# Two right-hand sums of a Strassen-Winograd down-projection formed on VectorE ahead of their store, instead of by adding DMA transfers ahead of their use

## The chip, the cores and the metric

The kernel runs on one core of a Trainium2 chip. The metric is the device time of one execution in microseconds (us). Times are medians of a few runs; profiles are of one execution each. The engines are named as in the profile: PE is TensorE's matmul and PEld its weight load, DVE is VectorE, ACT is ScalarE, POOL is GpSimd, SP is SyncE, which here only issues DMA transfers.

## The reference, cut to what matters

The model has two layers on an input of 1024 frames by 1024 channels, in float32. Each layer has a mixer and then a gated MLP with a short convolution. The change touches the MLP only:

```python
def conv_ffn(h, w_up, conv_w, conv_b, w_down):
    u = h @ w_up                                   # 1024 x 5632
    up = jnp.pad(u, ((0, 0), (CONV_WIDTH - 1, 0), (0, 0)))
    conv = conv_b
    for j in range(CONV_WIDTH):                    # width 3, along the frames
        conv = conv + conv_w[j] * up[:, j:j + s]
    a, g = jnp.split(conv, 2, axis=-1)
    return (jax.nn.silu(a) * g) @ w_down           # (1024 x 2816) @ (2816 x 1024)
```

The result is added to the residual stream.

## The kernel before, in words

Everything is held with channels on the 128 partitions and the 1024 frames along a row. A float32 matmul is made of three: each operand is split into a high part, rounded by a ScalarE copy, and a low part, a VectorE subtraction, and high times high, high times low and low times high are accumulated. Such a split is one ScalarE and one VectorE instruction (`split_block`, L1193 to L1197, for one 128x512 block).

**Up-projection** (`ffn`, L1011 on). The 2816 hidden channels are 22 tiles of 128. For tile i the kernel computes a pair, the `a` tile and the `g` tile, by one level of the Strassen-Winograd scheme: seven products instead of eight (`Pair`, L966 to L1005: P1, P5, P6, P2, P7, P4, P3, twelve 128x512 matmuls each), and VectorE adds that build the four output quarters (L990, L995, L1001, L1005) and scale them (L964). L1005 needs the end of P3; P3 accumulates into a bank that L995 must have read. VectorE and ScalarE also prepare the next pair's weights (L907 to L918), and then the convolution of the finished pair runs on ScalarE (L1038) and VectorE (L1039, L1041), followed by SiLU (L1171) and the product with the gate. The pairs 0 and 1 are computed plainly.

**What the down-projection needs.** It also uses the Strassen-Winograd scheme. Hidden tiles 2j and 2j + 1 form a block row j, with the two halves of the frames as block columns: B11 and B12 from the even tile, B21 and B22 from the odd one. The right-hand sides of the seven products are B11, T1 = B12 - B11, T2 = T3 + B11, T3 = B22 - B12, B22, T4 = T2 - B21, and B21. The end of each pair (L1174 to L1188) computes what is stored to device memory. An even pair leaves the product in `even` (L1175), T1 (L1176), and stores B11 and T1. An odd pair leaves B21 and B22 in `ca` (L1182), U = B11 - B21 in the first half of `cg` (L1183) and T3 in the second half (L1184), and stores `ca` (`b2`, L1186) and `cg` (`ut3`, L1187), 512 KB each. `even` is a single buffer; `ca` and `cg` come from three buffers used in turn. T2 and T4 are stored nowhere: T2 is T3 + B11, and T4 is T3 + U.

**Down-projection** (`down`, L1199 on). The order of the work is (product, j) with j from 0 to 10 inside and the products P1, P5, P6, P3, P7, P4 outside: six phases of eleven steps, 66 steps a layer, each of twelve 128x512 matmuls (`step`, L1260 to L1267). A last part with plain matmuls finishes the rows that need the seventh product. A step's operands are made by `prep` (L1243), called three steps ahead (`LEAD`, L1299): `fetched` (L1209) loads the right-hand block into one of four `rb` buffers from SP, and, where `right` (L1241) lists two sources, issues a second transfer from GpSimd that adds the second source to what has landed (L1213). That is so in P6 (T3, then B11) and in P4 (T3, then U). The left-hand block is made by `left` (L1218) from weights, in part kept from earlier phases. Both blocks are split by `split_block`. Between the steps further transfers are issued: residual rows (`load_x`), in P6 at j = 2 and j = 6 two groups of weights for the last part (`last_left`, L1287, 512 KB and 192 KB each), and in P7 and P4 the B21 blocks (`last_right`, L1275).

**What sets the order.** TensorE's instructions, and in the down-projection SP's too, stand in the order of the program. On the other engines a planner at build time orders them with a simulated timeline; each engine then runs its own list in order and waits on semaphores.

Of the kernel before, what the change touches and what calls it, by code (L numbers as in the profile page):

```python
# [12 lines left out]
F32 = mybir.dt.float32  # L13
R32 = mybir.dt.float32r
AF = mybir.ActivationFunctionType
ALU = mybir.AluOpType

P = 128
T = 1024
# [38 lines left out]
def trunk_kernel(  # L58
# [22 lines left out]
    nc = tc.nc  # L81
    V, S, G, PE = nc.vector, nc.scalar, nc.gpsimd, nc.tensor
# [9 lines left out]
    dram = ctx.enter_context(tc.tile_pool(name="dram", bufs=1, space=bass.MemoryType.DRAM))  # L92

    def slot(dtype, name):
        return xpool.tile([P, T], dtype, tag="x", name=name)
# [915 lines left out]
    def ffn(layer, nm, after, ow, mixt, onward=None):  # L1011
# [5 lines left out]
        T0, T1 = HALVES  # L1017
# [18 lines left out]
        def conv(m, u, c):  # L1036
            b = C_CONV + (layer * 2 * FT + m) * 4
            S.activation(c, u, AF.Identity, scale=pcol(b + 2), bias=pcol(b + 3))  # L1038
            V.scalar_tensor_tensor(c[:, 1:], u[:, :T - 1], pcol(b + 1), c[:, 1:],  # L1039
                                   op0=ALU.mult, op1=ALU.add)  # L1040
            V.scalar_tensor_tensor(c[:, 2:], u[:, :T - 2], pcol(b), c[:, 2:],  # L1041
                                   op0=ALU.mult, op1=ALU.add)
# [63 lines left out]
        even = slot(F32, "even")  # L1106
        cs_ = [slot(F32, "c") for _ in range(3)]
        blocks = []
        ready = []

        def first_down():

            raw = wpool.tile([P, T], F32, tag="wraw", name="wraw", bufs=1)
            for j, t in enumerate((w.raw_g, s12, s34, raw)):
                nc.sync.dma_start(t[:, T0], wdn[layer, 2 * j][:, T0])
                nc.sync.dma_start(t[:, T1], blocks[j]["B11"])
                ready.append((split_block(t[:, T0]), split_block(t[:, T1])))

        for i in range(FT):
            nx = i + 1 < FT  # L1120
            ca, cg = cs_[2 * i % 3], cs_[(2 * i + 1) % 3]
            if i == 0:
                ua, ug = us[0], us[1]
            elif i == 1:
                ua, ug = us[2], us[0]
                for cs, b in zip(HALVES, ps):
                    V.tensor_tensor(ug[:, cs], b, rstd_bc[:, cs], op=ALU.mult)
            else:
                further = i + 2 < FT
                if i == 2:  # L1130
                    p = Pair(i)
                    p.P1()
                ua, ug = p.ua, p.ug
                if not nx:
                    first_down()
                p.P5()
                if nx:
                    sums(i + 1)
                    split_a11(i + 1)
                if further:  # L1140
                    load_a(i + 2)
                p.P6()
                if nx:
                    split_s12()
                p.P2()
                scaled(ua[:, T0], T0)
                p.P7()
                scaled(ug[:, T1], T1)
                p.P4()
                p.D21()  # L1150
                if nx:
                    split_a22()
                if further:
                    load_g(i + 2)
                scaled(ug[:, T0], T0)
                q, p = p, None
                if nx:
                    p = Pair(i + 1)
                    p.P1()
                q.P3()  # L1160
                if nx:
                    split_s34()
                if further:
                    load_s4(i + 2)
                scaled(ua[:, T1], T1)
            if i == 1:
                for ld in loads:
                    ld(i + 2)
            conv(FT + i, ug, cg)
            conv(i, ua, ca)  # L1170
            S.activation(ca, ca, AF.Silu)  # L1171


            if i % 2 == 0:  # L1174
                V.tensor_tensor(even, ca, cg, op=ALU.mult)  # L1175
                V.tensor_tensor(ca[:, T0], even[:, T1], even[:, T0], op=ALU.subtract)  # L1176
                b11, t1 = (dram.tile([P, 512], F32, tag=f"{n}{layer}_{i}", name=n) for n in ("b11", "t1"))
                nc.sync.dma_start(b11, even[:, T0])
                nc.sync.dma_start(t1, ca[:, T0])
                blocks.append({"B11": b11, "T1": t1})  # L1180
            else:
                V.tensor_tensor(ca, ca, cg, op=ALU.mult)  # L1182
                V.tensor_tensor(cg[:, T0], even[:, T0], ca[:, T0], op=ALU.subtract)  # L1183
                V.tensor_tensor(cg[:, T1], ca[:, T1], even[:, T1], op=ALU.subtract)  # L1184
                b2, ut3 = (dram.tile([P, T], F32, tag=f"{n}{layer}_{i}", name=n) for n in ("b2", "ut3"))
                nc.sync.dma_start(b2, ca)  # L1186
                nc.sync.dma_start(ut3, cg)  # L1187
                blocks[-1].update(B21=b2[:, T0], B22=b2[:, T1], U=ut3[:, T0], T3=ut3[:, T1])  # L1188
        ev.close()

        down(layer, blocks, ready, after, onward)

    def split_block(src):  # L1193
        t = hpool.tile([P, T], R32, tag="h", name="blk")
        S.copy(t[:, 0:512], src)  # L1195
        V.tensor_sub(t[:, 512:T], src, t[:, 0:512].bitcast(F32))  # L1196
        return t  # L1197

    def down(layer, blocks, ready, after, onward):  # L1199
# [5 lines left out]
        T0, T1 = HALVES  # L1205
        NJ = FT // 2
        w = [(wdn[layer, 2 * j], wdn[layer, 2 * j + 1]) for j in range(NJ)]

        def fetched(tag, src, add=None, bufs=4):  # L1209
            t = dn.tile([P, 544 if tag == "rb" else 512], F32, tag=tag, name=tag, bufs=bufs)[:, 0:src.free_size()]  # L1210
            nc.sync.dma_start(t, src)
            if add is not None:
                G.dma_start(t, add, accum_op=ALU.add)  # L1213
            return t

        a11, s = [None] * NJ, [None] * NJ

        def left(n, j):  # L1218

            (lo_, hi_) = w[j]  # L1220
            if n == "P1":
                return a11[j]
            if n == "P5":
                s[j] = fetched("rs", hi_[:, T1], bufs=NJ)
                t = fetched("rw", lo_[:, T1])
                V.tensor_tensor(s[j], s[j], t, op=ALU.add)
                return s[j]
            if n == "P6":
                V.tensor_tensor(s[j], s[j], a11[j], op=ALU.subtract)
                return s[j]  # L1230
            if n == "P4":
                return fetched("rw", hi_[:, T1])
            t = fetched("rw", hi_[:, T0] if n == "P3" else lo_[:, T1])
            if n == "P3":
                V.tensor_tensor(t, t, s[j], op=ALU.subtract)
            else:
                V.tensor_tensor(t, a11[j], t, op=ALU.subtract)
            return t


        right = {"P1": ("B11",), "P5": ("T1",), "P6": ("T3", "B11"), "P3": ("B22",), "P7": ("T3",), "P4": ("T3", "U")}  # L1241

        def prep(n, j):  # L1243
            if n == "P1" and j < len(ready):
                return ready[j]
            rb = fetched("rb", *(blocks[j][b] for b in right[n]))
            if n == "P1":
                load_a11(j)
            return split_block(left(n, j)), split_block(rb)

        def load_a11(j):
            a11[j] = fetched("ra", w[j][0][:, T0], bufs=NJ)
# [50 lines left out]
        for n, j in order[:LEAD]:  # L1303
            ops[n, j] = prep(n, j)
# [55 lines left out]
        if onward is not None:  # L1360
            with norm.behind():
                n = wov0.shape[2]
# [25 lines left out]

    norm.sq_tile = lambda: slot(F32, "nsq")
    ffn(0, n0, lambda m: norm.add(x[m], HALVES if m == KT // 2 - 1 else None, m), ws, [mix[k] for k in last], onward)  # L1390


    ev = ExitStack()
    op = ev.enter_context(tc.tile_pool(name="odd", bufs=1, reuse_waits="tile"))
# [235 lines left out]
    for hd in range(GH):  # L1630
# [36 lines left out]

    nnorm = NormBlocks(1, C_FFN1, lambda: slot(F32, "nacc"), lambda: slot(F32, "nsq"))
    ffn(1, nnorm, lambda m: [nc.sync.dma_start(yT[m * P:(m + 1) * P, cs], x[m][:, cs]) for cs in HALVES],
        ow, mixt)  # L1670

# [63 lines left out]
```

## Time and profile before

| | |
|---|---|
| median of 3 runs | 2199.06 us (2197.35 to 2202.14) |
| the profiled execution's own time | 2199.35 us |
| its span in the profile | 2197.7 us |
| mean granted TensorE clock | 0.996 |
| up-projection pairs, layer 0 / layer 1 | about 483 to 881 us / 1571 to 1968 us |
| six down-projection phases, layer 0 / layer 1 | 881.4 to 1071.3 us / 1968.5 to 2162.4 us |
| bytes moved by DMA | 280.3 MB in 126,201 packets |

All times inside the run are counted from the span's start. In a group's row the numbers behind `x` are the count, the busy time in us and the mean of one in ns, then the engine's idle time just before the group and who ended it. In a timeline the columns are start, length, engine, line, operation, output and inputs; a bracket gives the idle time before it and its releaser. In a list of DMA issues the last number is the median time from issue to landing in us. A matmul of 512 columns shows some 390 ns, but successive ones overlap.

### The profile page before, as it was taken

How to read it: one execution, taken by the hardware profiler on the slowest of the kernel's cores; microseconds unless marked ns; L12 is line 12 of the kernel's file. 1: busy time of each engine (PE TensorE's matmuls, PEld its weight loads, DVE VectorE, ACT ScalarE, POOL GpSimd, SP SyncE). 2: the span in 40 equal slices, each digit the busy share in tenths (PEclk: the TensorE clock that was granted, in tenths of full speed). 3: DMA queues.
4: the chain of work that ended last, by engine and by line, in shares of the span. 5: the costliest groups of instructions: out<-in, count | busy, mean ns of one | idle time of the engine just before them, and what ended most of it. 6: DMA issues, size and time to landing. Idle time of an engine off the chain costs nothing.

```text
span 2197.7 us, 28082 instructions
## 1 busy us (share of the span) xinstructions
PE 2150.8 (98%) x10384; PEld 1767.0 (80%) x10384; DVE 1664.8 (76%) x2458; ACT 1093.1 (50%) x1705; POOL 162.1 (7%) x188
## 2 busy tenths in 40 slices
PE   8999989999999999999999999999999999999998
PEld 7889878888878888778887878787788888887776
DVE  5687688698989899777736655557898998987763
ACT  6666566464444444344546362637544444443441
POOL 2240120000000000010000000000000000000110
PEclk9999999999999999999999999999999999999999
DMA  4132332353444434987501111105343444449885
GB/s 152 49 107 87 94 112 94 119 130 106 130 119 126 124 116 124 350 216 233 169 21 40 38 49 38 49 30 145 105 124 116 123 122 120 124 157 327 222 239 157
DMA packets 126201, 280.31 MB, mean 128 GB/s; under 512 B 13408, under 2 KB 27360, under 8 KB 126064
## 3 DMA queue, kind: packets, MB, share of 16 engines
q1 hardware_dynamic: 112528, 251.25, 34.9%
q0 software_dynamic: 13536, 27.27, 7.0%
q8 instruction: 81, 1.33, 0.2%
q14 instruction: 56, 0.46, 0.1%
HBM read 208.21 MB, written 54.53 MB: 120 GB/s over the span
## 4 chain that ended last, share of the span: by engine, by line
PE 61%; DMA 15%; DVE 15%; issue 4%; ACT 4%; SPq 1%; POOL 0%; DVEq 0%; ACTq 0%; POOLq 0%
PE lin L936 10%; PE z L936 7%; PE lin L153 4%; PE lin L155 4%; PE lin L157 4%; DMA rb<-ut 4%; PE t L936 3%; PE d L936 3%; DMA rw<-in_wdn 3%; DVE blk L1196 2%; PE z L157 2%; PE z L153 2%; PE z L155 2%; DMA raw_g<-in_wup 2%; DMA wraw<-in_wup 2%
## 5 line engine op out<-in xcount | busy, mean ns | idle before, releaser
L1038 ACT ACTIVATE c<-u,prm 128x1024 f32<-128x1024 f32 x88 | 109.1, 1244 | 86.7 <-DVE u L964 79.1
L1266 PE MATMUL lin<-blk 128*128 128x512 f32 x396 | 118.6, 400 | 14.0 <-ACT blk L1195 8.6
L1196 DVE TENSOR_TENSOR blk<-rb,blk 128x512 fp32r<-128x512 f32 x124 | 85.1, 686 | 53.9 <-ACT blk L1195 53.4
L153 PE MATMUL lin<-h_hi,whi 128*128 128x512 f32 x288 | 114.2, 432 | 6.6 <-ACT whi L139 6.0
L1039 DVE SCALAR_TENSOR_TENSOR c<-u,prm,c 128x1023 f32<-128x1023 f32 x88 | 112.3, 1278 | 8.5 <-ACT c L1038 8.5
L1195 ACT CAST blk<-rb 128x512 fp32r<-128x512 f32 x124 | 76.6, 618 | 81.2 <-DMA rb<-ut 44.0
L936 PE MATMUL d<-T,a 128*128 128x512 f32 x480 | 115.4, 389 | 0.0
L1041 DVE SCALAR_TENSOR_TENSOR c<-u,prm,c 128x1022 f32<-128x1022 f32 x88 | 112.3, 1276 | 0.0
L1266 PE MATMUL t<-blk 128*128 128x512 f32 x396 | 112.0, 391 | 0.0
L1266 PE MATMUL d<-blk 128*128 128x512 f32 x396 | 111.9, 391 | 0.0
L1266 PE MATMUL z<-blk 128*128 128x512 f32 x396 | 111.6, 390 | 0.0
L964 DVE TENSOR_TENSOR u<-u,rstd_bc 128x512 f32<-128x512 f32 x160 | 107.8, 684 | 0.4
L936 PEld LDWEIGHTS d<-T,a 128*128 128x128 f32 x480 | 90.1, 188 | 18.7
L155 PE MATMUL lin<-h_lo,whi 128*128 128x512 f32 x288 | 104.4, 398 | 0.7 <-DVE h_lo L264 0.7
L1266 PEld LDWEIGHTS lin<-blk 128*128 128x128 f32 x396 | 73.0, 189 | 39.8 <-ACT blk L1195 13.2
L157 PE MATMUL lin<-h_hi,wlo 128*128 128x512 f32 x288 | 104.2, 398 | 0.0
L936 PE MATMUL z<-blk,s34h 128*128 128x512 f32 x320 | 101.3, 398 | 1.4 <-DVE u L995 1.4
L936 PE MATMUL z<-blk,s12h 128*128 128x512 f32 x320 | 100.9, 396 | 0.0
L936 PE MATMUL lin<-T,s34h 128*128 128x512 f32 x320 | 99.5, 392 | 0.8 <-ACT tm L986 0.8
L936 PE MATMUL t<-blk,whi 128*128 128x512 f32 x320 | 99.6, 392 | 0.0
L936 PE MATMUL lin<-blk,whi 128*128 128x512 f32 x320 | 99.5, 392 | 0.0
L936 PE MATMUL lin<-T,s12h 128*128 128x512 f32 x320 | 99.4, 391 | 0.0
(516 smaller groups left out, 6021.0 us busy)
## 6 DMA issues: line engine op xcount, KB each, us to landing
wraw<-in_wup SPq DMA_DIRECT2D x44, 512.0 KB, 3.7
rw<-in_wdn SPq DMA_DIRECT2D x88, 256.0 KB, 4.7
raw_g<-in_wup SPq DMA_DIRECT2D x40, 512.0 KB, 3.8
rb<-ut SPq DMA_DIRECT2D x66, 256.0 KB, 4.4
b<-c SPq DMA_DIRECT2D x22, 512.0 KB, 2.6
ut<-c SPq DMA_DIRECT2D x22, 512.0 KB, 3.8
s<-in_wup SPq DMA_DIRECT2D x40, 256.0 KB, 2.6
s<-s POOLq DMA_DIRECT2D x40, 256.0 KB, 4.4
```

Of the source, the lines that this page charges most:

```text
L153: PE.matmul(out[i], wh, ah[i], start=first, stop=False)
L155: PE.matmul(out[i], wh, al[i], start=False, stop=False)
L157: PE.matmul(out[i], wl, ah[i], start=False, stop=last)
L936: PE.matmul(ps, w, m, start=first and k == 0 and n == 0, stop=k == 3 and n == 2, skip_group_check=True)
L964: V.tensor_tensor(dst, dst, rstd_bc[:, cs], op=ALU.mult)
L1038: S.activation(c, u, AF.Identity, scale=pcol(b + 2), bias=pcol(b + 3))
L1039: V.scalar_tensor_tensor(c[:, 1:], u[:, :T - 1], pcol(b + 1), c[:, 1:], op0=ALU.mult, op1=ALU.add)
L1041: V.scalar_tensor_tensor(c[:, 2:], u[:, :T - 2], pcol(b), c[:, 2:], op0=ALU.mult, op1=ALU.add)
L1195: S.copy(t[:, 0:512], src)
L1196: V.tensor_sub(t[:, 512:T], src, t[:, 0:512].bitcast(F32))
L1266: PE.matmul(ps, l, m, start=first and j == 0 and i == 0, stop=j == NJ - 1 and i == 2, skip_group_check=True)
```

## The change

T2 and T4 are formed on VectorE at the end of each odd pair, where U and T3 have just been made. `cg` then holds T4 beside T3 and is stored as `t43`. T2 is formed in place in the first half of `even` and stored as a further 256 KB tensor, `t2`. In the down-projection every product has one right-hand source, and `fetched` loses its adding transfer. The sums have the same terms as before.

```diff
                 V.tensor_tensor(cg[:, T0], even[:, T0], ca[:, T0], op=ALU.subtract)
                 V.tensor_tensor(cg[:, T1], ca[:, T1], even[:, T1], op=ALU.subtract)
-                b2, ut3 = (dram.tile([P, T], F32, tag=f"{n}{layer}_{i}", name=n) for n in ("b2", "ut3"))
+                V.tensor_tensor(cg[:, T0], cg[:, T0], cg[:, T1], op=ALU.add)
+                V.tensor_tensor(even[:, T0], even[:, T0], cg[:, T1], op=ALU.add)
+                b2, t43, t2 = (dram.tile([P, n], F32, tag=f"{s}{layer}_{i}", name=s)
+                               for s, n in (("b2", T), ("t43", T), ("t2", 512)))
                 nc.sync.dma_start(b2, ca)
-                nc.sync.dma_start(ut3, cg)
-                blocks[-1].update(B21=b2[:, T0], B22=b2[:, T1], U=ut3[:, T0], T3=ut3[:, T1])
+                nc.sync.dma_start(t43, cg)
+                nc.sync.dma_start(t2, even[:, T0])
+                blocks[-1].update(B21=b2[:, T0], B22=b2[:, T1], T4=t43[:, T0], T3=t43[:, T1], T2=t2)
...
-        def fetched(tag, src, add=None, bufs=4):
+        def fetched(tag, src, bufs=4):
             t = dn.tile([P, 544 if tag == "rb" else 512], F32, tag=tag, name=tag, bufs=bufs)[:, 0:src.free_size()]
             nc.sync.dma_start(t, src)
-            if add is not None:
-                G.dma_start(t, add, accum_op=ALU.add)
             return t
...
-        right = {"P1": ("B11",), "P5": ("T1",), "P6": ("T3", "B11"), "P3": ("B22",), "P7": ("T3",), "P4": ("T3", "U")}
+        right = {"P1": "B11", "P5": "T1", "P6": "T2", "P3": "B22", "P7": "T3", "P4": "T4"}
...
-            rb = fetched("rb", *(blocks[j][b] for b in right[n]))
+            rb = fetched("rb", blocks[j][right[n]])
```

## Prediction

> **What bounds the kernel.** I read the head of the profile page first, then the matmul timeline of the two down-projections, the table of stretches cut at their phase borders, the list of DMAs and, last, VectorE's timeline in an up-projection.
>
> ```profile
> span 2197.7 us, 28082 instructions
> PE 2150.8 (98%) x10384; PEld 1767.0 (80%) x10384; DVE 1664.8 (76%) x2458; ACT 1093.1 (50%) x1705; POOL 162.1 (7%) x188
> L1266 PE MATMUL lin<-blk 128*128 128x512 f32 x396 | 118.6, 400 | 14.0 <-ACT blk L1195 8.6 <-DVE blk L1196 5.4
> ```
>
> TensorE is busy for all but 47 us, so a gain has to come out of matmuls that wait or run slowly. The costliest matmul group is L1266, the down-projections' step, and its waits are for `split_block` (L1195, L1196). Below, each row is one phase of eleven steps (132 matmuls): first P1, P5, P6, P3, P4 of layer 0, then P5, P6, P3, P4 of layer 1. A phase ends where the next one's first matmul starts. The columns are the length, the busy time (and instructions) of PE, PEld, DVE, ACT and POOL, the granted clock, the DMA share and GB/s.
>
> ```profile
> 881.36:911.30 29.94, 29.94 (x134) 24.77 (x132) 21.39 (x31) 12.23 (x19) 0.00 (x0) 1.00 0.98 344
> 911.30:943.80 32.50, 31.58 (x134) 24.30 (x132) 28.30 (x46) 13.09 (x23) 2.46 (x3) 1.00 0.92 311
> 943.80:980.81 37.01, 33.26 (x133) 25.70 (x132) 22.49 (x35) 17.12 (x30) 7.09 (x9) 0.95 0.93 225
> 980.81:1010.73 29.92, 29.92 (x133) 24.77 (x132) 26.09 (x43) 15.89 (x28) 0.00 (x0) 1.00 0.69 223
> 1040.65:1071.27 30.62, 30.40 (x133) 24.70 (x132) 23.44 (x38) 15.30 (x28) 5.79 (x7) 1.00 0.94 260
> 1998.47:2030.41 31.94, 31.21 (x134) 24.39 (x132) 27.74 (x46) 12.65 (x23) 2.60 (x3) 1.00 0.92 318
> 2030.41:2066.53 36.12, 31.65 (x134) 24.54 (x132) 21.28 (x33) 16.22 (x28) 6.92 (x8) 1.00 0.87 214
> 2066.53:2096.45 29.92, 29.92 (x133) 24.77 (x132) 26.23 (x43) 15.78 (x28) 0.00 (x0) 1.00 0.70 227
> 2126.37:2162.43 36.06, 32.20 (x134) 24.45 (x132) 24.38 (x39) 15.58 (x28) 6.05 (x7) 1.00 0.86 234
> ```
>
> P3 is the yardstick: 29.92 us, so 2.72 us a step, without a wait. P6 and P4 do the same matmuls and take longer, and these are the two phases whose right-hand sum is made by an adding transfer. Their DMA engines are nearly as full as in P1 while they move a third less. The next rows say why. The first four are of 945 to 980 us: queue, packets, megabytes, share of the engines, then the issues with KB and time to landing. The other four are of the whole run.
>
> ```profile
> q1 hardware_dynamic: 5077, 5.46, 52.9%
> q0 software_dynamic: 1280, 2.33, 40.1%
> rb<-b POOLq DMA_DIRECT2D x8, 256.0 KB, 6.2
> wraw<-in_wdn SPq DMA_DIRECT2D x2, 512.0 KB, 7.8
> rb<-ut SPq DMA_DIRECT2D x66, 256.0 KB, 4.4
> L1213 POOL DMA_DIRECT2D rb<-b x22 | 19.1, 880 | 213.7 <-DVE rs L1229 86.5 <-DVE blk L1196 86.2 <-DMA rb<-ut 36.8
> L1195 ACT CAST blk<-rb 128x512 fp32r<-128x512 f32 x124 | 76.6, 618 | 81.2 <-DMA rb<-ut 44.0 <-DMA rb<-b 33.5 <-PE d L1266 2.1
> L1196 DVE TENSOR_TENSOR blk<-rb,blk 128x512 fp32r<-128x512 f32 x124 | 85.1, 686 | 53.9 <-ACT blk L1195 53.4
> ```
>
> The adding transfers take 40.1% of the engines for 2.33 MB where plain ones take 52.9% for 5.46 MB: 1.8 times the price per byte. They also come one behind another. An `rb` buffer is held for the load (4.4), GpSimd's issue (0.9), the adding transfer (6.2) and the two halves of the split (0.6 and 0.7): 12.8 us. Four buffers give 3.2 us a step against TensorE's 2.72. Eleven steps would lose 11 x 0.48 = 5.3 us, about what P6 and layer 1's P4 lose.
>
> **What goes in the down-projections.** All 44 adding transfers go (11 steps, P6 and P4, two layers), with GpSimd's 0.9 us issues; GpSimd has nothing else there. A buffer is then held for 4.4 + 1.3 = 5.7 us, or 1.4 us a step. P6 fetches one 256 KB block a step, less than P3 does; P4 fetches a weight and a right-hand block as P3 does, and B21 blocks in some steps. If both came to P3's length they would give back 7.09 + 6.20 in P6 and 0.70 + 6.14 in P4: **20.1 us**, the upper end.
>
> Part of that is a slow clock, not waiting (the first row is SP's):
>
> ```profile
> 959.42 0.39 SPq L1293 DMA_DIRECT2D wraw<-in_wdn  x1
> 967.46 0.84 PE L1266 MATMUL d<-blk 128*128 128x512 f32 x3
> 970.39 0.50 PE L1266 MATMUL lin<-blk 128*128 128x512 f32 x1 [2.08 <-ACT blk L1195]
> 971.70 0.99 PE L1266 MATMUL z<-blk 128*128 128x512 f32 x3
> 972.48 1.49 PE L1266 MATMUL t<-blk 128*128 128x512 f32 x3
> 973.76 1.49 PE L1266 MATMUL d<-blk 128*128 128x512 f32 x3
> 975.04 1.17 PE L1266 MATMUL lin<-blk 128*128 128x512 f32 x3
> 976.05 0.85 PE L1266 MATMUL z<-blk 128*128 128x512 f32 x3
> ```
>
> After the 2.08 us gap three matmuls take 1.28 us from start to start instead of a quarter step's 0.68, and with the groups beside them 1.63 us are lost. I count them as following from the gap. The Trainium skill, TensorE: Matmul & The Clock Gate, section on the HAM clock gate, says the clock falls after an idle window of about 3.4 us; by that a 2.08 us gap is too short, the 1.63 us have another cause and may stay, and the upper end is 18.5 us. The trace shows the slow matmuls right behind the gap, and goes by it.
>
> Not all of the 20.1 need come. In P6 `last_left` puts two pairs of 512 and 192 KB loads on SP's queue ahead of `rb`, and the 2.08 us gap comes 11 us after the second of them (959.42). A block behind them comes some 3 us late (7.8 against 4.4). The three steps of lead are 8.2 us; a load and its split take 5.7, so 2.5 of the 3 are covered: 0.5 us a call without help from the fuller buffers. I take 1.5 us for all four calls; bounds 0 and 6, the latter if a call costs half its lateness.
>
> The last T2 is written while the down-projection's P1 fills the engines to 0.98 at 344 GB/s; 256 KB are 0.8 us. P5, which already waits 2.6 and 2.0 us over 29.92, would wait that much more. I take 1.5 us for both layers; bounds 0 and 3. The rest of P5's waits stays.
>
> **What is added in the up-projections.** Per odd pair two 128x512 adds, 44 in all, and one 256 KB store. What follows is an odd pair's end in layer 0 on VectorE, with SP's issues and TensorE's P3 of the next pair.
>
> ```profile
> 667.61 0.68 DVE L1183 TENSOR_TENSOR c<-even,c 128x512 f32<-128x512 f32 x1
> 668.22 0.68 DVE L1184 TENSOR_TENSOR c<-c,even 128x512 f32<-128x512 f32 x1
> 668.82 0.68 DVE L964 TENSOR_TENSOR u<-u,rstd_bc 128x512 f32<-128x512 f32 x1
> 670.93 0.69 DVE L1005 TENSOR_TENSOR u<-tm,z 128x512 f32<-128x512 f32 x1 [1.43 <-PE z L936]
> 682.31 1.22 DVE L1175 TENSOR_TENSOR even<-c 128x1024 f32<-128x1024 f32 x1
> 685.86 0.69 DVE L995 TENSOR_TENSOR u<-tm,z 128x512 f32<-128x512 f32 x1
> 667.72 0.33 SPq L895 DMA_DIRECT2D raw_g<-in_wup  x1
> 668.93 0.33 SPq L1187 DMA_DIRECT2D ut<-c  x1
> 675.78 0.33 SPq L902 DMA_DIRECT2D s<-in_wup  x1
> 687.33 0.63 PE L936 MATMUL z<-blk,s34h 128*128 128x512 f32 x2
> 592.19 0.69 DVE L1005 TENSOR_TENSOR u<-tm,z 128x512 f32<-128x512 f32 x1 [0.72 <-PE z L936]
> 593.32 0.69 DVE L907 TENSOR_TENSOR s<-raw_g 128x512 f32<-128x512 f32 x1 [0.44 <-DMA raw_g<-in_wup]
> ```
>
> A 0.68 us add delays the next instruction by 0.60 (667.61 to 668.22 to 668.82), so two cost 1.2 us an odd pair, 26.4 in all. They become ready right after L1184, and VectorE then waits 1.43 us at L1005 for P3's bank. So that wait hides them. At the tightest odd pair seen (592.19) it is 0.72, with 0.44 more at L907: 1.16 us, so under 0.1 spills. Behind the new adds on VectorE stand L964 or L1005; L964 can slip by 1.2 us without moving L1005. If the cover were gone, the next deadline is L995: it ends at 686.55, and P3 needs its bank at 687.33, so a lag of up to 0.8 us would still cost TensorE nothing. I take 1 us for both layers; bounds 0 and 26.4. The value is near zero because the nearest row, the 1.43 us wait, lies directly behind.
>
> The Trainium skill, VectorE: DVE Perf Modes, section The DRAIN you can't avoid, speaks against this: the next instruction does not start until the pipeline has emptied, so an add would cost its full 0.68, 30 us in all, and 1.36 an odd pair. That spills 0.2 us at the tightest pair, a sum some 1 us worse. The starts 0.60 apart disagree, and the measurement decides.
>
> On SP the `t2` store comes behind `t43`, itself 0.6 us later than `ut`; the next issue is at 675.78, and the `raw_g` load has gone before. The store must have read `even` before L1175 overwrites it at 682.31: issued near 671, and at the 4.4 us of a load, it is done 7 us ahead.
>
> **Sum.** -20.1 + 1.5 + 1.5 + 1 = -16.1 us against the profiled execution's 2199.35, and the median of 2199.06 stands 0.3 below that: **2183 us**.
>
> **Rivals.**
> 1. *P6 keeps its waits behind `last_left`.* For it: the 2.08 us gap. Against: P3 carries two plain loads a step without a wait. It keeps the 6 us bound and P5's 3: -20.1 + 6 + 3 + 1 = -10, 2189 us.
> 2. *The adds come in the wrong place.* The planner sets VectorE's order. If they stand behind L1005, the next pair is 1.2 us late, 0.4 beyond L995's slack, in 20 odd pairs: 8 us. 2183 + 7 = 2190 us.
> 3. *Slower: VectorE becomes the bound of the up-projection.* If the adds, or the wait for `t2` before L1175, are never covered, all 26.4 us fall on TensorE: 2183 + 25.4 = 2208 us. It decides from 0.8 us lost per odd pair (16.1 + 1 over 22). For it: VectorE is the second busiest engine. Against: the 1.43 and 1.16 us of waiting.
> 4. *The adding is not what P6 and P4 wait for.* For it: P4 of layer 0 loses 0.70 only, at a DMA share of 0.94 and with the same adding transfers. Against: P3. Nothing would come back, and the added work would cost 1.5 + 1: 2201.5 us.
>
> The change cannot fail to do what it says: T2 and T4 are stored ready, and `fetched` has no second transfer left.
>
> **Numbers.** Forecast 0.72, rival 1 0.08, rival 2 0.10, rival 3 0.06, rival 4 0.04. About 0.2% (4.4 us) is what can be told from no change. Forecast, 1 and 2 are faster, less 0.02 for rivals 1 and 2 together reaching into no change: 0.88. Rival 3 is slower: 0.06. Rival 4 lies within 4.4 us of no change, which with the 0.02 gives 0.06. Low end: all 20.1 us and half of P5's 4.6: 2199 - 22.4, so 2177. High end: rivals 1 and 2 with 2 to 3 us more: 2193.
>
> **What would show it.** Right: no adding transfers on GpSimd in the down-projections; P6 and P4 at 29.9 to 31 us each; DMA share in P6 under 0.75; an up-projection as long as before, and the wait before L1005 in odd pairs near 0.2 us. Wrong: P6 still at 36 us (the adding was not the cause); new waits of P3 for L995, of L1175 for `t2`, or of `raw_g` loads in the up-projections (rivals 2 and 3); P5 above 33.5 us.

## The result, and the profile after

The kernel after the change takes 2180.4 us (median, 2177.5 to 2181.4) where the kernel before takes 2198.2 us (2195.6 to 2202.1): a ratio of 0.9915, 95% interval 0.9897 to 0.9934. That is 17.8 us; 16.1 were forecast. In a second set of runs the same pair gave 2174.69 against 2198.04 us, ratio 0.9895 (0.9874 to 0.9915). The intervals overlap, so the gain is some 18 to 23 us.

The profiled execution took 2181.4 us. The head of its page and the costliest matmul group (L1267 was L1266) read:

```profile
span 2179.7 us, 28102 instructions
PE 2143.2 (98%) x10384; PEld 1767.2 (81%) x10384; DVE 1689.6 (78%) x2502; ACT 1094.8 (50%) x1705; POOL 123.7 (6%) x144
L1267 PE MATMUL lin<-blk 128*128 128x512 f32 x396 | 113.8, 392 | 1.8 <-DVE blk L1200 1.8
```

The group, the first quarter of each step, lost 4.8 us of busy time and 12.2 us of waiting. VectorE has 44 instructions more, GpSimd 44 fewer. Next, the table of stretches cut at the phase borders, with the same columns as in the prediction: P5, P6, P3, P4 of layer 0, then P5, P6, P3, P4 of layer 1.

```profile
911.55:944.24 32.69, 31.58 (x134) 24.31 (x133) 28.55 (x47) 14.99 (x27) 0.00 (x0) 1.00 0.86 298
944.24:974.15 29.91, 29.91 (x133) 24.77 (x132) 25.05 (x41) 16.41 (x30) 0.00 (x0) 1.00 0.78 241
974.15:1004.07 29.92, 29.92 (x133) 24.77 (x132) 24.11 (x40) 14.05 (x25) 0.00 (x0) 1.00 0.60 194
1033.99:1063.91 29.92, 29.92 (x133) 24.77 (x132) 18.45 (x30) 12.12 (x22) 0.00 (x0) 1.00 0.54 171
1992.77:2024.63 31.86, 31.13 (x133) 24.46 (x132) 27.72 (x46) 15.09 (x27) 0.00 (x0) 1.00 0.83 295
2024.63:2054.55 29.92, 29.92 (x133) 24.77 (x132) 26.65 (x43) 17.70 (x31) 0.00 (x0) 1.00 0.76 243
2054.55:2084.47 29.92, 29.92 (x133) 24.77 (x132) 24.31 (x40) 12.67 (x23) 0.00 (x0) 1.00 0.66 212
2114.39:2144.31 29.92, 29.92 (x133) 24.77 (x132) 17.39 (x29) 9.66 (x17) 0.00 (x0) 1.00 0.50 158
```

P6 and P4 run at TensorE's own pace in both layers, and the slow clock in P6 (0.95 before) is gone with its gap. From profile to profile the span falls by 18.0 us, and this is where:

| part | us |
|---|---|
| P6: 37.01 to 29.91, 36.12 to 29.92 | -13.3 |
| P4: 30.62 to 29.92, 36.06 to 29.92 | -6.8 |
| P5: 32.50 to 32.69, 31.94 to 31.86 | +0.1 |
| start of the first down-projection, 881.36 to 881.61 | +0.25 |
| from the end of its P4 to layer 1's down-projection, 897.23 to 898.92 | +1.7 |
| the tail after layer 1's P4, 35.27 to 35.39 | +0.1 |

The list of DMAs from 945 to 974 us shows what fills P6 now: queue, packets, MB, share of the engines; then issues with KB and time to landing.

```profile
q1 hardware_dynamic: 5988, 7.10, 78.1%
rb<-b SPq DMA_DIRECT2D x8, 256.0 KB, 4.9
rb<-t SPq DMA_DIRECT2D x5, 256.0 KB, 3.9
```

Before, plain transfers took 52.9% for 5.46 MB there and adding ones 40.1% for 2.33 MB, 3.4 and 6.0 us of engine time per MB (share times 35 us over MB). Now it is 3.2 us (78.1% of 29 us over 7.10 MB) for all.

In the up-projection, an odd pair's end on VectorE in layer 0, and SP's issues beside it:

```profile
665.97 0.69 DVE L1184 TENSOR_TENSOR c<-c,even 128x512 f32<-128x512 f32 x1
667.17 1.29 DVE L964 TENSOR_TENSOR u<-u,rstd_bc 128x512 f32<-128x512 f32 x2
668.38 0.68 DVE L1185 TENSOR_TENSOR c<-c 128x512 f32<-128x512 f32 x1
668.98 0.69 DVE L1186 TENSOR_TENSOR even<-even,c 128x512 f32<-128x512 f32 x1
669.92 0.69 DVE L1005 TENSOR_TENSOR u<-tm,z 128x512 f32<-128x512 f32 x1 [0.25 <-PE z L936]
689.32 0.69 DVE L1005 TENSOR_TENSOR u<-tm,z 128x512 f32<-128x512 f32 x1 [1.92 <-PE z L936]
669.09 0.33 SPq L1190 DMA_DIRECT2D t<-c  x1
669.69 0.33 SPq L1191 DMA_DIRECT2D t<-even  x1
```

The adds (L1185, L1186) stand behind L964 and ahead of L1005, 0.60 us apart, and the wait before L1005 shrank from 1.43 to 0.25 us: the time of the two adds came out of it. In all twenty odd pairs with an L1005 behind them they stand ahead of it. The even pair behind still has 1.92 us. TensorE lost no time by them: from the start of layer 1's first seven-product pair to its down-projection it took 378.27 us before (1590.23 to 1968.50) and 378.25 after (1584.58 to 1962.83).

### The profile page after: what moved, and what is told of

Its sections match the earlier page's. It is cut to its first block, busy times and chain, and to the rows that moved or that the text cites. A ratio compares the mean times of both kernels' runs of the same rounds, so it can differ in the third digit from the quotient of the medians.

```text
span 2179.7 us, 28102 instructions
## 1 busy us (share of the span) xinstructions
PE 2143.2 (98%) x10384; PEld 1767.2 (81%) x10384; DVE 1689.6 (78%) x2502; ACT 1094.8 (50%) x1705; POOL 123.7 (6%) x144
## 3 DMA queue, kind: packets, MB, share of 16 engines
q1 hardware_dynamic: 115696, 257.02, 36.2%
## 4 chain that ended last, share of the span: by engine, by line
PE 80%; DMA 6%; DVE 6%; ACT 4%; issue 2%; SPq 1%; POOL 0%; DVEq 0%; ACTq 0%; POOLq 0%
PE lin L936 14%; PE z L936 10%; PE d L936 5%; PE t L936 5%; PE lin L153 4%; PE lin L155 4%; PE lin L157 4%; PE lin L1267 3%; PE z L1267 3%; PE t L1267 3%; PE d L1267 3%; PE z L157 2%; PE z L153 2%; PE z L155 2%; DMA x<-xs 1%
## 5 line engine op out<-in xcount | busy, mean ns | idle before, releaser
L1267 PE MATMUL lin<-blk 128*128 128x512 f32 x396 | 113.8, 392 | 1.8 <-DVE blk L1200 1.8
L1267 PE MATMUL z<-blk 128*128 128x512 f32 x396 | 111.4, 389 | 0.0
L1267 PE MATMUL t<-blk 128*128 128x512 f32 x396 | 111.2, 389 | 0.0
L1267 PE MATMUL d<-blk 128*128 128x512 f32 x396 | 111.2, 389 | 0.0
L964 DVE TENSOR_TENSOR u<-u,rstd_bc 128x512 f32<-128x512 f32 x160 | 108.1, 686 | 0.6
L139 ACT CAST whi<-wraw 128x1024 fp32r<-128x1024 f32 (+2 forms) x57 | 57.2, 1003 | 83.6 <-PE z L155 21.9
L1267 PEld LDWEIGHTS lin<-blk 128*128 128x128 f32 x396 | 73.5, 188 | 20.7 <-DVE blk L1200 5.7
L1267 PEld LDWEIGHTS z<-blk 128*128 128x128 f32 x396 | 74.3, 188 | 15.6
```

Of the source, the lines that this page charges most:

```text
L139: S.copy(hi[:, cs], raw[:, cs])
L964: V.tensor_tensor(dst, dst, rstd_bc[:, cs], op=ALU.mult)
L1267: PE.matmul(ps, l, m, start=first and j == 0 and i == 0, stop=j == NJ - 1 and i == 2, skip_group_check=True)
```

## The experiments

Theory of the prediction, "holding": an adding transfer keeps one of four `rb` buffers for 12.8 us, so the loads come at 3.2 us a step. Rival, "engine time": adding transfers fill the DMA engines, and more buffers wouldn't help. Where a row is shown without a remark, it is of the table of stretches.

**More buffers (before, eight for P6).** Odd steps of P6 take their right-hand block from the four `rw` buffers, which P6 leaves unused.

```diff
-            rb = fetched("rb", *(blocks[j][b] for b in right[n]))
+            rb = fetched("rw" if n == "P6" and j % 2 else "rb", *(blocks[j][b] for b in right[n]))
```

> The kernel before, but in P6 every second right-hand block goes into one of the four `rw` buffers, which P6 doesn't use, so that eight buffers take turns there instead of four; the adding transfers stay. Holding theory (an `rb` buffer is held 12.8 us, and four of them give 3.2 us a step): 12.8 / 8 = 1.6 us a step, P6 falls from 37.0 and 36.1 us to 30 to 31 us, P4 stays at 30.6 and 36.1; 2198 - 12 = 2186 us. Rival, engine time (the adding transfers simply fill the DMA engines): a step of P6 costs the engines 0.87 us for the load and 1.58 us for the adding transfer, eleven steps 27 us, and `last_left` some 6 us more, so P6 can't go below 33 us whatever the buffers; 2198 - 6 = 2192 us or no change.

2193.73 us against 2196.22, ratio 0.9990 (0.9978 to 1.0002). P6 in both layers, and below it the list of DMAs from 944 to 979 us:

```profile
943.75:979.11 35.36, 32.13 (x134) 25.86 (x132) 25.72 (x41) 18.90 (x33) 6.09 (x7) 0.95 0.94 251
2028.45:2064.63 36.18, 33.25 (x133) 26.59 (x132) 27.14 (x43) 20.27 (x35) 6.09 (x7) 0.91 0.92 248
```

```profile
rb<-b POOLq DMA_DIRECT2D x4, 256.0 KB, 7.2
rb<-ut SPq DMA_DIRECT2D x3, 256.0 KB, 9.1
```

With twice the buffers P6 is no better than 35.4 and 36.2 us. The loads start sooner and land later: 9.1 us for a plain `rb` load, 5.5 in the same stretch before, and 7.2 for an adding one instead of 6.2. But TensorE waits in each layer at the start of one step of P6 alone (2.34 and 0.89 us in layer 0), and this is what stands behind the 2.34, on TensorE, ScalarE and GpSimd:

```profile
951.69 0.50 PE L1266 MATMUL lin<-blk 128*128 128x512 f32 x1 [2.34 <-ACT blk L1195]
949.65 1.04 ACT L1294 CAST whi<-wraw 128x1024 fp32r<-128x1024 f32 x1 [4.04 <-DMA wraw<-in_wdn]
951.02 0.61 ACT L1195 CAST blk<-rb 128x512 fp32r<-128x512 f32 x1
938.82 0.86 POOL L1213 DMA_DIRECT2D rb<-b  x1 [0.94 <-DMA rw<-ut]
```

The adding transfer of this block, issued at 938.82, landed 7.8 us later, at 946.6. ScalarE rounded the block at 951.02 only: in its list `last_left`'s cast (L1294) stands ahead, and that waited for a 512 KB load of weights, issued at 938.90, that took 10.7 us. The matmuls behind the wait run as slowly as behind the 2.08 us gap of before (1.28 us for three). Layer 1 is alike: one such wait of 2.63 us, behind a load that took 10.7 us. So holding is not the whole loss, since with enough buffers P6 still loses 5.4 us. But the run does not make the engines' time P6's floor either: its last adding transfer (961.58) landed 10 us before P6's end. What is left with eight buffers is a load of weights that comes late among fuller engines, and an engine that takes its work in a fixed order.

**Fewer buffers (before, three `rb`).**

```diff
-            t = dn.tile([P, 544 if tag == "rb" else 512], F32, tag=tag, name=tag, bufs=bufs)[:, 0:src.free_size()]
+            t = dn.tile([P, 544 if tag == "rb" else 512], F32, tag=tag, name=tag, bufs=3 if tag == "rb" else bufs)[:, 0:src.free_size()]
```

> The kernel before with three `rb` buffers instead of four, in all phases. Holding theory: 12.8 / 3 = 4.27 us a step in P6 and P4, 17 us lost a phase instead of 5.3, some 12 us more in three or four phases, 2235 to 2245 us; P3 and P7 stay at 29.9 us (5.7 / 3 = 1.9 us a step). Engine time: the engines have the same to do, P6 and P4 within 2 us of before, 2198 to 2203 us.

2247.7 us, ratio 1.0238 (1.0216 to 1.0260). P6 and P4 of layer 0:

```profile
943.53:987.28 43.75, 36.47 (x133) 26.21 (x133) 20.84 (x33) 15.09 (x26) 7.81 (x9) 0.92 0.76 174
1049.89:1096.68 46.79, 37.40 (x132) 27.41 (x133) 27.99 (x45) 19.58 (x35) 7.79 (x9) 0.89 0.83 215
```

Here the share falls to 0.76 and 0.83: the engines are not full, the buffers are the limit. Three buffers held 12.8 us give 4.27 us a step, 17 us over in eleven; P6 loses 13.8 over 29.92. P5, P3 and P7 of layer 0 grew too, to 35.45, 31.31 and 31.30 us, where the last two had been expected at 29.9. So holding is a real limit: it sets the pace with three buffers, and with four it lies close to TensorE's 2.72 us a step.

**The second source by a plain transfer (before, P6's sum made on VectorE in the down-projection).** The bytes stay the same, only the adding goes.

```diff
-            rb = fetched("rb", *(blocks[j][b] for b in right[n]))
+            rb = fetched("rb", *(blocks[j][b] for b in right[n][:1 if n == "P6" else 2]))
+            if n == "P6":
+                V.tensor_tensor(rb, rb, fetched("rw", blocks[j]["B11"]), op=ALU.add)
```

> The kernel before, but in P6 the second source is loaded by a plain transfer into an `rw` buffer and added on VectorE in the down-projection; P4 keeps its adding transfers. Holding theory: both loads run side by side, 4.4 + 0.7 + 1.3 = 6.4 us a buffer, 1.6 us a step, and VectorE has four instructions at 0.60, 2.4 us a step, below 2.72: P6 at 30 to 31.5 us, 2186 to 2188 us. Engine time: two plain loads cost 1.7 us a step where the pair cost 2.45, P6 also near 30. Rival, VectorE: with `last_left`'s two splits (some 3.2 us) its 26.4 us fill P6 to 29.6 of 29.9, and P6 stays at 32 us or more.

2183.5 us, ratio 0.9943 (0.9926 to 0.9961). P6:

```profile
941.45:971.47 30.02, 30.02 (x133) 24.70 (x132) 27.15 (x44) 15.93 (x27) 0.00 (x0) 1.00 0.78 247
2022.43:2053.10 30.67, 30.24 (x133) 24.70 (x132) 26.75 (x43) 15.82 (x27) 0.00 (x0) 1.00 0.76 241
```

So it is the adding that costs P6 its time, not the bytes of a second source. (The second source has `rw` buffers of its own here, but the run with eight buffers had those too and kept its loss.) P4, left as it was, took 32.55 and 32.87 us.

**T2 alone by the change (P4 keeps its adding transfer).** Of the change's diff only T2's add and store and P6's entry in `right`:

```diff
+                V.tensor_tensor(even[:, T0], even[:, T0], cg[:, T1], op=ALU.add)
...
+                nc.sync.dma_start(t2, even[:, T0])
...
+        right = {"P1": ("B11",), "P5": ("T1",), "P6": ("T2",), "P3": ("B22",), "P7": ("T3",), "P4": ("T3", "U")}
```

> Half of the change: T2 is formed and stored in the up-projections and P6 loads it; U is stored as before and P4 keeps its adding transfers. All theories that put the waits down to the adding transfers: P6 at 29.9 us in both layers, P4 as before or, in layer 0, up to 5 us worse since P6's late start no longer lets P4's loads run ahead; 2198 - 13.3 + 1 = 2186 us. If the two halves interact (a shared queue on GpSimd or a full set of engines at the phase borders): P6 keeps 2 us or more.

2184.17 us, ratio 0.9949 (0.9931 to 0.9968). P6 took 29.93 and 29.92 us; P4 kept its loss:

```profile
1033.54:1065.46 31.92, 31.04 (x133) 24.53 (x132) 24.33 (x40) 16.51 (x30) 5.83 (x7) 1.00 0.94 250
2113.71:2147.36 33.65, 31.20 (x133) 24.54 (x132) 22.74 (x37) 14.45 (x26) 5.73 (x7) 1.00 0.85 226
```

The two halves of the change act each on its own phase. P4's loss differs from run to run by some us (0.70 and 6.14 in the profile before, 2.00 and 3.73 here), so how the 20.1 us split between P6 and P4 is that profile's.

**The last part's weights out of P6 (before, `last_left` in P3).**

```diff
-            if n == "P6" and j in (2, 6):
+            if n == "P3" and j in (2, 6):
```

> The kernel before with `last_left`'s loads for the first two rows moved from P6 to P3, at the same j. Engine time: without them P6's adding transfers and loads need 27 us of the engines in 29.9, so P6 falls from 37.0 and 36.1 us to 30 to 31 us; P3, whose engines were 0.69 busy, takes them in and stays at 29.9; 2198 - 12 = 2186 us. Holding theory: four buffers still allow one step in 3.2 us, P6 stays at 35 us and loses 5 us; 2198 - 3 = 2195 us. Rival 1 of the prediction in its plain form (the losses are `last_left`'s alone, the adding is harmless): P6 exactly at 29.9 us.

2197.68 against 2197.91 us, ratio 1.0005 (0.9994 to 1.0017). P6, P3 and P4 of layer 0:

```profile
940.11:971.32 31.21, 30.72 (x133) 24.62 (x132) 17.40 (x28) 12.80 (x24) 6.93 (x8) 1.00 0.85 193
971.32:1003.41 32.09, 30.53 (x134) 24.62 (x132) 26.95 (x43) 16.20 (x28) 0.00 (x0) 1.00 0.71 230
1033.91:1071.55 37.64, 33.35 (x133) 24.33 (x133) 27.88 (x45) 19.27 (x35) 6.90 (x8) 1.00 0.93 255
```

Without these 1.4 MB and their splits P6 falls from 37.0 to 31.2 us (in layer 1 from 36.1 to 30.7) with the adding transfers still there and the same four buffers. Holding at 3.2 us a step would have kept it at 35, but the time that a buffer is held is not fixed: from an `rb` load of P6 to the fourth behind it, which takes the same buffer, it was 12.4 to 15.4 us in the filled middle of P6 before (loads from 939.91 to 953.04) and 10.4 to 12.3 us here (936.21 to 948.55). So P6's loss needed both, the adding transfers and the weights beside them. But the waits only moved: P6 gained 5.8 us, P3 lost 2.2, P7 0.6 and P4 7.0. Why P4 lost as much was not pursued.

**The added work without its use (before, both adds and the store in the up-projections; the down-projection as before, so that P4's sum takes T4 for U).**

```diff
+                V.tensor_tensor(cg[:, T0], cg[:, T0], cg[:, T1], op=ALU.add)
+                V.tensor_tensor(even[:, T0], even[:, T0], cg[:, T1], op=ALU.add)
...
+                nc.sync.dma_start(t2, even[:, T0])
```

> The kernel before with the changed up-projection alone: the two adds and the stores of the odd pairs as in the change, while the down-projection keeps its adding transfers (P4 then adds T3 to T4 instead of U, and T2 is stored for nobody). Theory (the adds lie in VectorE's wait before L1005): the up-projections as long as before to 1 us each, and the down-projections as before but for 1 us from the added store; 2197 to 2200 us. Rival 2: 8 us more, 2206 us. Rival 3: 26 us more, 2224 us.

2197.35 against 2197.91 us, ratio 1.0003 (0.9991 to 1.0014): the adds and the store cost nothing that can be measured, and P6 (35.53 and 35.04 us) keeps its loss. The gain is all in the removal.

**The change without its adds (P6 uses B11, P4 uses U).**

```diff
-                V.tensor_tensor(cg[:, T0], cg[:, T0], cg[:, T1], op=ALU.add)
-                V.tensor_tensor(even[:, T0], even[:, T0], cg[:, T1], op=ALU.add)
```

> The changed kernel without the two VectorE adds: the transfers are the same, but P6's right-hand side is B11 instead of T2 and P4's is U instead of T4. Theory: the adds are hidden, so nothing is saved; 2179 to 2181 us, as the changed kernel. If the adds cost on the path, this is faster by that: 2172 us by rival 2's 8 us.

2175.71 us, ratio 0.9907 (0.9886 to 0.9927), not to be told from the kernel after. Layer 1's stretch from the first seven-product pair to the down-projection is 377.64 us (1577.38 to 1955.02) against 378.25; in layer 0, from one wait ahead of the MLP (424.58 to 876.62, against 429.11 to 881.61), it is 452.04 against 452.50. So the adds cost 0.61 + 0.46 = 1.1 us in the traces; the prediction took 1.

**Four more adds (after).** The adds are repeated twice, so T4 and T2 hold other sums.

```diff
+                for _ in range(2):
+                    V.tensor_tensor(cg[:, T0], cg[:, T0], cg[:, T1], op=ALU.add)
+                    V.tensor_tensor(even[:, T0], even[:, T0], cg[:, T1], op=ALU.add)
```

> The kernel after the change, with four more VectorE adds behind the two in each odd pair of the up-projection: the two adds repeated twice, so T4 and T2 as stored hold other sums (that part of the computation is changed). It tells how far VectorE's cover reaches, on which the prediction put 1 us and bounds 0 and 26.4. Four more adds are 4 x 0.60 = 2.4 us an odd pair, 53 us of VectorE in all. My theory: the idle time of VectorE over two pairs is the cover; in the kernel after the change it was 0.25 us before L1005 in an odd pair and 1.92 us in the next even pair, 2.17 in all, and TensorE has 0.8 us of slack at L995 that absorbs the first lag. 2.4 us against 2.17 leave 0.2 us an odd pair over, so 20 odd pairs x 0.2 = 4 to 5 us slower than the kernel after: 2184 to 2190 us. The rival, that an added VectorE instruction falls on TensorE once the wait directly before L1005 is used up: 20 x (2.4 - 0.25 - 0.8) = 27 us, 2205 to 2210 us; with no slack at L995 either, 2223 us and more. A third, that VectorE has more cover than these two waits show: 2180 us, no difference. The down-projections stay at 29.9 us in P6 and P4 in each.

2189.69 us, ratio 0.9963 (0.9947 to 0.9978). The first row is the up-projection's stretch from 510 to 872 us, the other one of TensorE's timeline.

```profile
510.00:872.00 362.00, 358.85 (x1551) 290.71 (x1551) 356.61 (x456) 162.20 (x187) 15.47 (x18) 1.00 0.43 130
```

```profile
572.01 0.74 PE L936 MATMUL z<-blk,s34h 128*128 128x512 f32 x2 [1.05 <-DVE u L995]
```

VectorE is now busy for 356.6 of 362 us (339.5 in the kernel after, 326.7 before). TensorE waits for L995 by 1.04 to 1.16 us at eight places, four in each layer (two in the kernel after, 0.34 and 1.01 us), and the two up-projections are 4.1 and 4.0 us longer than in the kernel after: 8.1 us for 53 us of adds. The cover ends between two and six adds, and where it ends, TensorE waits where the prediction put the next deadline, at L995's bank.

**What P5 still waits for.** In the kernel after, VectorE's timeline in P5 shows a step of 3.26 us:

```profile
905.50 0.69 DVE L1228 TENSOR_TENSOR rs<-rs,rw 128x512 f32<-128x512 f32 x1 [2.62 <-DMA rw<-in_wdn]
...
923.58 0.69 DVE L1228 TENSOR_TENSOR rs<-rs,rw 128x512 f32<-128x512 f32 x1
925.03 0.69 DVE L1200 TENSOR_TENSOR blk<-rs,blk 128x512 fp32r<-128x512 f32 x1 [0.76 <-ACT blk L1199]
925.64 0.69 DVE L1200 TENSOR_TENSOR blk<-rb,blk 128x512 fp32r<-128x512 f32 x1
926.24 0.68 DVE L1231 TENSOR_TENSOR rs<-rs,ra 128x512 f32<-128x512 f32 x1
926.85 0.69 DVE L1228 TENSOR_TENSOR rs<-rs,rw 128x512 f32<-128x512 f32 x1
```

VectorE sums the left-hand block (L1228), waits 0.76 us for ScalarE to round that sum, makes the two low parts and then does P6's subtraction (L1231, all eleven of them here). That is 3.26 us against TensorE's 2.72. It also starts late: the first sum waits 2.62 us for a load of weights and comes 23.9 us after P1's start. Two edits are meant to tell start and pace apart. The first splits the right-hand block ahead of the left-hand one (run twice, the second time beside the kernel after on the same chip):

```diff
-            return split_block(left(n, j)), split_block(rb)
+            rt = split_block(rb)
+            return split_block(left(n, j)), rt
```

> The changed kernel with the right-hand block split before the left-hand one is formed. In the changed kernel's P5 VectorE sums the left block, waits 0.76 us for ScalarE's copy of that very sum, and then splits: 3.26 us a step. With the right-hand split between the sum and its own split the wait is covered: P5 from 32.7 and 31.9 us to 30 to 30.5 us in both layers; 2180 - 4 = 2176 us. Rival: P5 waits for its three loads a step (DMA share 0.86 and 0.83 there), and stays at 32 us; 2180 us. Rival: the planner puts the splits in the old order whatever the program says: same profile, 2180 us.

> The kernel after the change with the right-hand block split ahead of the left-hand one, beside the kernel after on the same chip. In its first profile P5 lost 0 and 0.5 us instead of 2.8 and 1.9, with VectorE at 3.31 us a step as before but its first left-hand sum of P5 19.7 us after P1's start instead of 23.9. Theory: what P5 waits for is set by where VectorE starts (the loads that it waits for) and not by its pace alone, so P5 comes at 29.9 to 30.5 again and the kernel is 4 to 5 us faster than the kernel after. Rival: the earlier start was a chance of that one run; P5 at 31.9 and no difference.

> The kernel after the change itself, as the yardstick on the same chip for the two kernels sent with it. 2178 to 2182 us; P5 at 32.7 and 31.9 us as in its first profile, everything else in the down-projections at 29.9.

The first time 2173.18 us, ratio 0.9895 (0.9874 to 0.9916); the second 2174.32 us, ratio 0.9890 (0.9867 to 0.9914), beside 2174.69 us for the kernel after. P5 of the second:

```profile
911.89:941.81 29.92, 29.92 (x134) 24.78 (x132) 26.18 (x43) 14.09 (x26) 0.00 (x0) 1.00 0.81 296
1987.84:2018.27 30.43, 30.43 (x134) 24.63 (x132) 26.52 (x44) 13.93 (x25) 0.00 (x0) 1.00 0.81 295
```

P5's loss is gone both times, yet VectorE's step didn't get shorter: it still waits 0.69 us for ScalarE, and the sums are 3.31 us apart. What changed is the start, 19.7 and 20.5 us after P1's (the fifth sum comes 7.0 us into P5 instead of 8.8), and the order: the last low part of a step ends 2.06 us behind the start of the sum instead of 2.75. The time is no better than that of the kernel after, however. In the two profiles P5 gains 3.4 us (2.81 and 0.63), and 3.3 us are lost ahead of the first down-projection, most of them in the mixer (below). Whether P5's gain would show in the time with that loss away stays open.

The second edit takes L1231 off VectorE:

```diff
-                V.tensor_tensor(s[j], s[j], a11[j], op=ALU.subtract)
+                G.tensor_tensor(s[j], s[j], a11[j], op=ALU.subtract)
```

> The kernel after the change with P6's subtraction of the left-hand block (L1231) on GpSimd instead of VectorE. All eleven of them stand on VectorE inside P5 in the kernel after: 11 x 0.60 = 6.6 us, and P5's steps on VectorE are 3.26 us apart against TensorE's 2.72. If the pace matters as much as the start, VectorE's step falls to about 2.66 us and P5 to 29.9 to 30.5 us: 3.5 to 4.5 us faster than the kernel after. If only the late start matters (a wait of 2.6 us for a load of weights), P5 stays at 31.5 or more and the time is the same. Worse than the kernel after if GpSimd's subtraction is so long that P6 waits for it instead: P6 over 31 us.

2189.9 us, ratio 0.9965 (0.9953 to 0.9977): some 15 us slower than the kernel after on the same chip. P5, and then the timeline of GpSimd and VectorE:

```profile
910.85:948.55 37.70, 33.47 (x134) 24.23 (x132) 32.36 (x38) 15.14 (x27) 16.33 (x10) 1.00 0.74 260
1994.77:2032.41 37.64, 34.14 (x134) 25.56 (x132) 32.30 (x37) 15.76 (x29) 15.00 (x9) 0.95 0.74 256
```

```profile
919.30 1.67 POOL L1231 TENSOR_TENSOR rs<-rs,ra 128x512 f32<-128x512 f32 x1 [2.08 <-DMA x<-xs]
919.74 1.78 DVE L1228 TENSOR_TENSOR rs<-rs,rw 128x512 f32<-128x512 f32 x1
923.49 1.77 DVE L1228 TENSOR_TENSOR rs<-rs,rw 128x512 f32<-128x512 f32 x1
```

VectorE's step grew instead of shrinking, to 3.75 us, since its sum beside GpSimd's subtraction takes 1.78 us instead of 0.69. With 0.49 us a step more P5 lost 5.0 and 5.8 us more. So the pace counts as well as the start: P5 is a slow VectorE eating up the lead that it starts with.

## Why the prediction was right, point by point

- **The 20.1 us.** All came: 7.10 + 6.20 in P6, 0.70 + 6.14 in P4, to a hundredth of P3's length. This includes the 1.63 us of slow clock behind the 2.08 us gap. The rule that the prediction set against it, an idle window of about 3.4 us (the Trainium skill, TensorE: Matmul & The Clock Gate, section on the HAM clock gate), would have left them; they went with the gap.
- **The mechanism was half right.** The price of an adding transfer (1.8 times the engine time) and the held buffer were both named, but the sum of 11 x 0.48 took the held time as fixed and as the only limit. With the weights moved away the same four buffers gave 31.2 us. With eight buffers the wait that was left stood behind a load of weights that took 10.7 us and held up ScalarE. What the sum left out is that the adding transfers also make the other transfers late. How much of P6's 7.09 us is the one and how much the other was not measured apart.
- **`last_left`, 1.5 us: measured 0.** The lateness that it was sized from (7.8 us for a 512 KB load against 4.4 for one of 256 KB) was that of engines filled by adding transfers. Without them the 512 KB load lands in 5.5 us and an `rb` load in 3.9 to 4.9. The share in P6 is 0.78 and 0.76, not under 0.75 as forecast, and it did no harm.
- **The last `t2` store, 1.5 us in P5: measured +0.19 and -0.08.** The step failed in its cause: it took P5 for a phase that waits for transfers throughout. P5's first sum does (23.9 us after P1's start, 24.7 before, so not later for the store), but from then on VectorE's pace sets its length.
- **The adds, 1 us: 1.1 us in the traces** beside the kernel without them, and within 0.3 us of nothing beside the kernel before. They stand where the prediction put them, and the wait before L1005 is 0.24 to 0.28 us in twelve of the twenty odd pairs, for the 0.2 forecast. The tightest pair that the prediction saw was not the tightest: in layer 1, L1005 at 1757.25 waited for nothing before the change, and the next 1.26 us of VectorE's idle time came right behind it. The add's cost to VectorE is 0.60, as in the trace of before, not the whole 0.68 to 0.69 that the prediction took from the rule that an instruction waits for the pipeline to empty (the Trainium skill, VectorE: DVE Perf Modes, section The DRAIN you can't avoid, which also says that an instruction that is not held starts earlier).
- **Not foreseen: 1.7 us** between the two down-projections, in one profile. Of it 1.42 us is one wait in layer 1's mixer for a rounded weight (at 1405.40), and it isn't in the second profile of the same kernel, taken in the second set of runs. With the measured sizes the sum is -20.1 + 0.1 + 1.1 = -18.9 us, between the two measured gains of 17.8 and 23.4.
- **What was luck.** The twelve phases of the two down-projections took 383.84 us in the profile of before, 363.78 in the first and 363.05 in the second of the kernel after: 20.1 and 20.8 us less. What is left of the spans' differences, 2 us more in the first and 4 us less in the second, lies nearly all ahead of the down-projections, and most of it in waits of the mixers, which the change doesn't touch. So it is in part luck that 16.1 came so near 17.8: two charges of 1.5 us that were not there stood in for waits in the mixers. In the second set 2174.69 us lies below the low end of 2177.

Of the rivals, 1 would have shown waits in P6 and 4 no gain. Rivals 2 and 3 were about the right deadline, L995, but even at three times the adds TensorE paid 8 us, not the 25 of rival 3.

## What to carry to other kernels

A transfer that adds on its way in saves an instruction and pays with the DMA engines' time: look at the share of the engines per byte by queue before taking it as free, and put the sum where the engine that makes it is waiting anyway. The time that a buffer is held grows with what else is on the engines, so a sum of buffers and holding times is good only beside the transfers that it was read from. When a relief gives nothing, look at the wait that is left before naming the limit: with eight buffers it was another wait. Waits that are moved out of one phase are to be counted in all the others.

## What the runs showed of the hardware

**VectorE and GpSimd.** A 128x512 VectorE sum that starts 0.44 us into a GpSimd subtraction ends 0.55 us after it (919.74 + 1.78 against 919.30 + 1.67), as if it had to wait for its end. The Trainium skill, SBUF — State Buffer, section Who interferes with whom, says that a VectorE instruction with two SBUF inputs contends with a GpSimd instruction that reads SBUF; the trace agrees, with 1.78 us for 0.69.

**A gap in the mixer of layer 0.** In a part of the program that the change doesn't touch, the same matmul waits for 1.58 us in some executions and 0.54 in others. Here it is in two profiles of the kernel after, with the clock from 240.5 to 252 us (the column ahead of the last two):

```profile
241.24 0.38 PE L756 MATMUL d<-atl,vt 128*128 128x256 f32 x1 [1.58 <-DVE atl L744]
240.50:252.00 11.50, 10.76 (x49) 9.04 (x50) 7.22 (x16) 7.80 (x17) 2.40 (x1) 0.85 0.42 139
```

```profile
240.02 0.38 PE L756 MATMUL d<-atl,vt 128*128 128x256 f32 x1 [0.54 <-DVE atl L744]
240.50:252.00 11.50, 11.50 (x63) 9.70 (x63) 8.54 (x17) 7.60 (x16) 2.41 (x1) 1.00 0.47 165
```

Behind the long gap the granted clock is 0.85, behind the short one 1.00, and the next 25 us take 1.6 us more (26.5 against 24.9 to the next such wait). Together that is most of the 2.9 us by which the first down-projection starts earlier in the second profile (878.68 against 881.61). The profile of before has the long gap too, 1.57 us, so the first two profiles are compared alike. All fourteen profiles agree: behind the five gaps of 1.57 or 1.58 us the clock over the next 11 us is 0.84, and where the gap is 0.77 us or less it is 1.00. A gap of 1.42 us at 1405.40 in the kernel after was followed by a clock of 1.00; what else decides was not tried, and neither was why the gap is long or short.
